# Expert stages of a two-layer diffusion backbone: TensorE's work written out in a fixed order, with the sums and picks of the second layer split and placed between the products

## The chip, the cores and the metric

One core of one Trainium2 chip. The metric is the device time of one execution in microseconds, as the median of three runs. All data are float32.

## The reference

Two layers work on 512 latent tokens (`x`) and 256 context tokens (`ctx`) of width 1024. Each layer is a mixer (mLSTM in layer 0, retention in layer 1) and then an expert-choice mixture of experts, cut here to what the change touches:

```python
def expert_choice_ffn(h, router, w_gate, w_up, w_down):
    cap = CAPACITY_FACTOR * t // N_EXPERTS              # 64 latent, 32 context tokens
    aff = softmax(h @ router)
    gate, idx = lax.top_k(swapaxes(aff, 1, 2), cap)     # each expert takes its best tokens
    xs = h[bidx, idx]
    hid = silu(xs @ w_gate) * (xs @ w_up)
    y = (hid @ w_down) * gate[..., None]
    return zeros_like(h).at[bidx, idx].add(y)
...
x = x + mod_l[5] * expert_choice_ffn(h_lat, ...)        # both layers
ctx = ctx + mod_c[5] * expert_choice_ffn(h_ctx, ...)    # layer 0 only
```

There are 16 experts a layer, each with three 1024 x 1024 matrices (12 MB). The second layer's result goes through a last RMSNorm.

## The kernel before, in words

`moe(l, ...)` (L1199) is the expert stage of layer `l`; its loop over the experts begins at L1488. The program is written in some order, and a scheduler puts each engine's instructions in its own order, from modelled times and from what each instruction needs. Where a block is under `tc.manual_schedule(engines={PE})`, TensorE keeps the written order; the other engines are still scheduled. Before the change only the first expert's opening (L1466) and the last expert (L1496) of layer 1 are under it.

**Weights.** `load` (L1165) fetches a 1 MB piece (256 rows of a matrix) on SP's queue. Gate, up and down of an expert are four pieces each. The pieces go round 19 slots in layer 0 and 14 in layer 1, and a load waits until the product that read its slot's last piece is done.

**Products.** `prod` (L1276) streams the weights past the chosen tokens: 32 matmuls of 512 columns for the 64 latent tokens, 64 of 256 columns for the 32 context tokens. `gate_up` (L1408) makes `gl` or `ul` (latent), or one half of `cg` (context: gate and up share one PSUM tile); after gate ScalarE takes Silu into `hid` (L1425), after up VectorE multiplies it (L1427). `turn` (L1429) transposes `hid` on TensorE (`hp`) and copies it on ScalarE into `hT`; `down` (L1437) makes `y`.

**Layer 0.** Tokens come by indirect DMA on POOL (`gather`, two experts ahead, three buffers `xg`) and the results are added in DRAM by indirect DMA, also on POOL. `prep` (L1225) transposes the next expert's tokens (`xp`) and modulates them on VectorE (`xs`, L1253 and L1255). In program order an expert is: `gl`, `cg` gate, `ul`, `cg` up, gathers, `prep` of the next, `turn` latent and context, `down` latent and context.

**Layer 1** (latent alone) keeps the tokens in SBUF. `select` (L1209) makes a 0/1 matrix `pick` for two experts at a time (`chosen` on TensorE, `own` and `pick` on VectorE); `prep`, called in odd experts for the next two, multiplies it with the tokens' high and low parts (`xr`, L1235, eight matmuls for each half of the width), copies to `rows` on ScalarE, transposes (`xp`, L1247) and modulates. `rows` and `hT` share one buffer (tag `hT0`). `put_back` (L1289) collects two experts' results (`o`), splits them into `bh` and `bl` after each odd expert, makes `put` matrices on VectorE and then, in one loop over four token tiles and two halves, adds them to the tokens: 16 matmuls `back` (L1313) into two PSUM buffers, eight adds on VectorE (L1316).

`xr`, `xp`, `hp` and `chosen` share three PSUM buffers (tag `tp`).

Of the kernel before, what the change touches and what calls it, by code (L numbers as in the profile page):

```python
# [9 lines left out]
F32 = mybir.dt.float32  # L10
# [3 lines left out]
AF = mybir.ActivationFunctionType  # L14
OP = mybir.AluOpType
# [8 lines left out]
NE = 16  # L24
# [3 lines left out]
LAT, CTX = 0, 1  # L28
# [16 lines left out]
def backbone(ctx, tc, x, c, ctx_in, c_ctx, ada_w, ada_b, norm_mix_g, norm_ffn_g, final_norm_g,  # L45
# [3 lines left out]
    nc = tc.nc  # L49
# [12 lines left out]
    ident = consts.tile([128, 128], F32, name="ident")  # L62
# [138 lines left out]
    def behind(late, early):  # L201

        for a in late:
            tc.add_manual_dep(a.ins, early.ins.name, mybir.DependencyInfo(mybir.DependencyClass.NoSync,
                                                                  mybir.DependencyReason.DATA), reason="order")
# [991 lines left out]
            return [lambda k, m=m: ws[m, k // 2][:, k % 2] for m in range(3)]  # L1197

    def moe(l, R, sb, sbx, late, mp, ml):  # L1199
        two = l == 0  # L1200
        NT = 96 if two else 128
        SPAN = ((0, 64), (64, 96)) if two else ((0, 128),)
# [22 lines left out]
        def prep(e, xs, parts):  # L1225

            a, b = SPAN[parts[0]][0], SPAN[parts[-1]][1]
            if l:
                pick = select(e)
            for hh in range(2):  # L1230
                if l:
                    p = mp.tile([128, 512], F32, name="xr", tag="tp", bufs=3)
                    for t in range(4):
                        for part in (R.XH, R.XL):
                            nc.tensor.matmul(p, pick[:, t, :], part[t][:, hh * 512:hh * 512 + 512],  # L1235
                                             start=(t == 0 and part is R.XH), stop=(t == 3 and part is R.XL))
                    rows_ = sb.tile([128, 512], F32, name="rows", tag="hT0", bufs=1)
                    nc.scalar.activation(rows_, p, AF.Copy)
                p = mp.tile([128, 4, NT], F32, name="xp", tag="tp", bufs=3)
                for kk in range(4):  # L1240
                    ks = slice((hh * 4 + kk) * 128, (hh * 4 + kk + 1) * 128)
                    if l == 0:
                        LATE["xp"] = nc.tensor.transpose(p[:, kk, a:b], R.XG[e][a:b, ks], ident[a:b, a:b])
                        if LATE.get("hold"):
                            behind([LATE["xp"]], LATE["hold"])
                    else:
                        nc.tensor.transpose(p[:, kk, :], rows_[:, kk * 128:(kk + 1) * 128], ident)  # L1247
                s = slice(hh * 4, hh * 4 + 4)
                for v in parts:
                    c0, c1 = SPAN[v]  # L1250
                    n = c1 - c0
                    o = xs[:, s, c0:c1] if xs.shape[2] == NT else xs[:, s, :]
                    nc.vector.tensor_tensor(o, p[:, :, c0:c1],  # L1253
                                            gsc[l][1][:, s, v:v + 1].to_broadcast([128, 4, n]), op=OP.mult)
                    LATE["xs"] = nc.vector.tensor_tensor(o, o,  # L1255
                                            modcol[l][:, 24 + hh * 4:28 + hh * 4, v:v + 1].to_broadcast([128, 4, n]),
                                            op=OP.add)

        def prep_first(xs, *groups):

# [28 lines left out]
        def put_back(e, o):  # L1289


            odd = e % 2
            if not odd:
                for q in range(2):
                    BACK[q] = sbx.tile([128, 512], F32, name=f"o{q}", bufs=1)
            for h in range(2):
                hs = slice(64 * h, 64 * h + 64)
                nc.vector.scalar_tensor_tensor(BACK[h ^ odd][hs, :], o[hs, :], R.gcol[hs, e:e + 1], M5[odd][hs, :],
                                               op0=OP.mult, op1=OP.mult)
            if not odd:  # L1300
                return
            put, hi, lo = [], [], []
            for q in range(2):
                hi.append(sbx.tile([128, 512], F32R, name=f"bh{q}", bufs=1))
                lo.append(sbx.tile([128, 512], F32R, name=f"bl{q}", bufs=1))
                split_piece(hi[q], lo[q], BACK[q])
                put.append(sb.tile([128, T_LAT], F32R, name=f"put{q}", bufs=1))
                nc.vector.tensor_scalar(put[q], R.tok, R.pair[:, q, e // 2:e // 2 + 1], None, op0=OP.is_equal)
            for t in range(4):
                for q in range(2):  # L1310
                    p = mp.tile([128, 512], F32, name="back", bufs=2)
                    for part in (hi, lo):
                        nc.tensor.matmul(p, put[q][:, t * 128:(t + 1) * 128], part[q],  # L1313
                                         start=part is hi, stop=part is lo)
                    xq = R.X[t][:, q * 512:(q + 1) * 512]
                    nc.vector.tensor_tensor(xq, xq, p, op=OP.add)  # L1316

# [25 lines left out]
        def final_gain():  # L1343

            fg = R.slot()[:, 0, :]
            for h in range(2):
                p = mp.tile([128, 4, 128], F32, name="rbp", tag="tp", bufs=3)
                for cc in range(4):
                    nc.tensor.transpose(p[:, cc, :], vc1[:, 80 + h * 4 + cc:81 + h * 4 + cc].to_broadcast([128, 128]),
                                        ident)  # L1350
                nc.scalar.activation(fg[:, h * 512:(h + 1) * 512], p.rearrange("p a b -> p (a b)"), AF.Copy)
            return fg
# [55 lines left out]
        def gate_up(v, xs, what, w, steps=range(8)):  # L1408
# [17 lines left out]
            else:  # L1426
                nc.vector.tensor_tensor(HID[v], HID[v], o, op=OP.mult)  # L1427

        def turn(v):  # L1429
            nb = 4 >> v  # L1430
            p = mp.tile([128, nb, 128], F32, name="hp", tag="tp", bufs=3)
            for cc in range(nb):
                nc.tensor.transpose(p[:, cc, :], HID[v][:, cc * 128:(cc + 1) * 128], ident)  # L1433
            HT[v] = (late if v else sb).tile([128, nb, 128], F32, name=f"hT{v}", bufs=1)
            LATE["act"] = nc.scalar.activation(HT[v], p, AF.Copy)  # L1435

        def down(v, e, w):  # L1437
            cw, nb = 64 >> v, 4 >> v
# [46 lines left out]
                R.ctx(mp)  # L1485
        M5 = gate_rows(l, late, mb0, mp) if two else R.M5

        for e in range(NE):  # L1488
            wg, wu, wd = W
            if two and e not in (0, NE - 1):  # L1490
                gate_up(LAT, xs, 0, wg)
                gate_up(CTX, xs, 0, wg)
                gate_up(LAT, xs, 1, wu)
                gate_up(CTX, xs, 1, wu)
            elif l and e == NE - 1:
                with tc.manual_schedule(engines={mybir.EngineType.PE}):  # L1496
                    fg = final_gain()
                    for what, w in enumerate((wg, wu)):
                        for b in range(4):
                            gate_up(LAT, xs, what, w, range(2 * b, 2 * b + 2))  # L1500
                            next(BACK["steps"], None)
                    turn(LAT)
                    finish(fg)
            elif not l or e:
                gate_up(LAT, xs, 0, wg)
                gate_up(LAT, xs, 1, wu)
            if e + 1 < NE:
                W = weights(e + 1)
                if two or e % 2:
                    xn = sbx.tile([128, 8, NT], F32, name="xs", bufs=2 - l)  # L1510
            if two and e == 0:
                turn(LAT)
                down(LAT, e, wd)
                LATE["hold"] = LATE["pe"]
                prep(0, xs, (CTX,))
                del LATE["hold"]
            if two and e in (0, NE - 1):
                if e:
                    turn(LAT)
                    down(LAT, e, wd)  # L1520
                    xc = sb.tile([128, 8, 32], F32, name="xc", tag="hT0", bufs=1)
                    prep(e, xc, (CTX,))
                    xs = xc
                gate_up(CTX, xs, 0, wg)
                gate_up(CTX, xs, 1, wu)
            if l == 0 and e + 2 < NE:
                for v in streams:
                    R.gather(e + 2, v)
            if e + 1 < NE and (two or e % 2):
                prep(e + 1, xn, streams if e + 2 < NE else (LAT,))  # L1530
            if e not in (0, NE - 1) or l and e == 0:
                turn(LAT)
            if two:
                turn(CTX)
            if e not in (0, NE - 1) or l and e == 0:
                down(LAT, e, wd)
            if two:
                down(CTX, e, wd)
            if two or e % 2:
                xs = xn  # L1540


    kn_scale = float(np.float32(128 ** -0.5))
# [328 lines left out]
```

## Time and profile before

| | us |
|---|---|
| median of 3 runs (lowest, highest) | 1977.88 (1977.67, 1979.93) |
| the profiled execution's own time | 1974.15 |
| its span, first to last instruction | 1972.4 |
| TensorE busy, share of the span | 1850.9, 94% |
| VectorE, ScalarE, GpSimd busy | 730.2, 426.8, 279.8 |
| moved by DMA | 585.42 MB, mean 297 GB/s |

Matmuls overlap in the array and their ends are modelled, so a busy TensorE need not be one at its peak. "Idle before" names what ended the idle time. In the rows, PE is TensorE, PEld its weight load, DVE VectorE, ACT ScalarE, POOL GpSimd and SP the engine that issues most transfers; SPq is its queue's own wait. DMA share is the busy share of 16 DMA engines from the time that packets took, so it can pass 1.

### The profile page before, as it was taken

The page shows a single profiled execution, that of the slowest core. Times are in us where ns is not written, and L with a number is a line of the kernel's source. Part 1 is how long each engine was busy: PE and PEld are TensorE (multiplying, and loading weights), DVE is VectorE, ACT ScalarE, POOL GpSimd, SP SyncE. Part 2 cuts the span into 40 slices and gives each one's busy share as a digit, 9 for nine tenths or more (in the row PEclk, how much of TensorE's full clock was granted, in tenths as well). Part 3 has the DMA queues.
Part 4 walks back from the last instruction along what each step waited for, and adds up shares of the span by engine and source line. Part 5 has one row for each costly group of instructions (what it writes and reads, how often), then busy time and mean ns, then how long its engine had stood idle before and what let it go on. Part 6 is the DMA issues. An engine that isn't in the chain of part 4 may idle for free. (4 is left out here: it accounts for less than half of the span.)

```text
span 1972.4 us, 27775 instructions
## 1 busy us (share of the span) xinstructions
PE 1850.9 (94%) x11091; PEld 1012.6 (51%) x11091; DVE 730.2 (37%) x1739; ACT 426.8 (22%) x839; POOL 279.8 (14%) x340
## 2 busy tenths in 40 slices
PE   7999988999999999999998999999979999989997
PEld 2765766787344443333334777788754333333332
DVE  3544567546111110110104677355551322222223
ACT  3532355432000000000004522322411000000001
POOL 1111133301211121120011124144000000000001
PEclk9999999999999999999999999999979999999999
DMA  8567776764999999999984588354559999999992
GB/s 285 205 209 268 253 207 196 230 228 144 333 393 375 391 383 384 383 382 393 401 319 126 182 279 276 112 173 150 208 208 395 415 416 414 415 414 414 416 413 86
DMA packets 218258, 585.42 MB, mean 297 GB/s; under 512 B 17674, under 2 KB 69618, under 8 KB 213010
## 3 DMA queue, kind: packets, MB, share of 16 engines
q1 hardware_dynamic: 209840, 570.72, 77.6%
q0 software_dynamic: 6912, 12.71, 3.2%
q8 instruction: 88, 1.44, 0.3%
q10 hardware_dynamic: 1378, 0.23, 0.1%
q14 instruction: 40, 0.33, 0.0%
HBM read 544.13 MB, written 39.47 MB: 296 GB/s over the span
## 5 line engine op out<-in xcount | busy, mean ns | idle before, releaser
L1282 PE MATMUL y<-wslot,hT 128*32 128x256 f32 (+1 forms) x2016 | 291.1, 488 | 9.8 <-ACT hT L1435 9.6
L1282 PE MATMUL gl<-wslot,xs 128*64 128x512 f32 x1024 | 260.3, 610 | 0.8 <-DVE xs L1255 0.8
L1282 PE MATMUL ul<-wslot,xs 128*64 128x512 f32 x1024 | 239.3, 596 | 0.0
L290 PE MATMUL acc<-whi,hT_hi 128*128 128x512 f32 x544 | 223.2, 411 | 4.8 <-ACT hT_hi L360 3.1
L291 PE MATMUL acc<-wlo,hT_hi 128*128 128x512 f32 x544 | 217.6, 400 | 0.3 <-POOL wlo L297 0.3
L292 PE MATMUL acc<-whi,hT_lo 128*128 128x512 f32 x544 | 217.3, 399 | 0.2 <-DVE hT_lo L361 0.2
L1427 DVE TENSOR_TENSOR hid<-hid,ul 128x512 f32<-128x512 f32 x32 | 22.0, 688 | 463.5 <-PE ul L1282 463.5
L1282 PEld LDWEIGHTS y<-wslot,hT 128*32 128x32 f32 (+1 forms) x2016 | 100.2, 123 | 178.1 <-issue 137.3
L1282 PEld LDWEIGHTS ul<-wslot,xs 128*64 128x64 f32 x1024 | 72.2, 137 | 140.8 <-issue 136.2
L1282 PEld LDWEIGHTS gl<-wslot,xs 128*64 128x64 f32 x1024 | 69.4, 138 | 135.5 <-issue 131.1
L290 PEld LDWEIGHTS acc<-whi,hT_hi 128*128 128x128 f32 x544 | 102.8, 189 | 39.4 <-issue 9.8
L1282 PE MATMUL cg<-wslot,xs 128*32 128x256 f32 x1920 | 118.9, 382 | 0.5 <-ACT hid L1425 0.5
L292 PEld LDWEIGHTS acc<-whi,hT_lo 128*128 128x128 f32 x544 | 102.8, 189 | 28.5 <-issue 4.9
L291 PEld LDWEIGHTS acc<-wlo,hT_hi 128*128 128x128 f32 x544 | 103.2, 190 | 23.7 <-issue 2.4
L1425 ACT ACTIVATE hid<-gl 128x512 f32<-128x512 f32 x32 | 19.1, 597 | 439.6 <-PE gl L1282 439.6
L297 DVE TENSOR_TENSOR wlo<-wslot,whi 128x512 fp32r<-128x512 f32 x108 | 80.6, 762 | 56.1 <-ACT whi L296 55.8
L1282 PEld LDWEIGHTS cg<-wslot,xs 128*32 128x32 f32 x1920 | 56.5, 109 | 84.1 <-issue 51.1
L296 ACT ACTIVATE whi<-wslot 128x512 fp32r<-128x512 f32 x112 | 69.4, 630 | 99.2 <-PE acc L292 98.2
L1435 ACT ACTIVATE hT<-hp 128x512 f32<-128x512 f32 (+1 forms) x48 | 23.7, 524 | 297.4 <-PE hp L1433 297.4
L1387 POOL TENSOR_TENSOR wslot<-x,wslot 128x512 f32<-128x512 f32 x4 | 5.0, 1271 | 493.2 <-DVE x L1330 491.6
L290 PE MATMUL po<-woh,yh 128*128 128x512 f32 x160 | 64.5, 403 | 3.2 <-ACT yh L923 3.2
L1449 DVE SCALAR_TENSOR_TENSOR o<-y,gcol,M 128x512 f32<-128x512 f32 (+1 forms) x32 | 19.8, 617 | 125.8 <-PE y L1282 125.8
(440 smaller groups left out, 2449.9 us busy)
## 6 DMA issues: line engine op xcount, KB each, us to landing
wslot<-in_moe_w_up_dram SPq DMA_DIRECT2D x128, 1024.0 KB
wslot<-in_moe_w_gate_dram SPq DMA_DIRECT2D x128, 1024.0 KB
wslot<-in_moe_w_down_dram SPq DMA_DIRECT2D x124, 1024.0 KB
wslot<-in_ada_w_dram SPq DMA_DIRECT2D x40, 1024.0 KB
wslot<-in_ret_w_in_dram SPq DMA_DIRECT2D x16, 1024.0 KB
wslot<-in_mlstm_w_in_dram SPq DMA_DIRECT2D x12, 1024.0 KB
wslot<-in_ada_w_dram SPq DMA_DIRECT2D x16, 512.0 KB
E<-rows_d SPq DMA_DIRECT2D x24, 256.0 KB
```

The source lines that it names most:

```text
L290: nc.tensor.matmul(o, lh, rh, start=first, stop=False)
L291: nc.tensor.matmul(o, lh, rl, start=False, stop=False)
L292: nc.tensor.matmul(o, ll, rh, start=False, stop=last)
L296: nc.scalar.activation(wh, w, AF.Copy)
L297: eng.tensor_tensor(wl, w, wh.bitcast(F32), op=OP.subtract)
L1282: mm = nc.tensor.matmul(o[cw * q:cw * q + cw, :], stat(k), w(k)[:, qn * n:(qn + 1) * n], start=(k == 0), stop=(k == 7), tile_position=(0, ...
L1387: nc.gpsimd.tensor_tensor(O[:, lo], R.X[t][:, lo], fg[:, lo], op=OP.mult)
L1425: nc.scalar.activation(HID[v], o, AF.Silu)
L1427: nc.vector.tensor_tensor(HID[v], HID[v], o, op=OP.mult)
L1435: LATE["act"] = nc.scalar.activation(HT[v], p, AF.Copy)
L1449: LATE["dve"] = nc.vector.scalar_tensor_tensor(r, o, TOP[v][2][:, e:e + 1], M5[v], op0=OP.mult, op1=OP.mult)
```

## The change

TensorE keeps the written order in experts 1 to 14 of layer 0 and in all of layer 1. The order itself is rewritten. In layer 0 the context's up product comes before the latent one, and `turn` and `down` take the context first. In layer 1 `prep` is cut into `pick_rows` (one half's `xr` and `rows`) and `row_columns` (that half's `xp` and `xs`), the sums of `put_back` into `add_back(tiles)`, and `turn` into its transposes and its copy; odd experts have the picks between their products, even ones the sums. What is computed stays the same.

```diff
 def moe(l, R, sb, sbx, late, mp, ml):
+    ordered = tc.manual_schedule
+    PE_ONLY = {mybir.EngineType.PE}
...
+    def pick_rows(e, hh):
+        pick = select(e)
+        p = mp.tile([128, 512], F32, name="xr", tag="tp", bufs=3)
+        for t in range(4):
+            for part in (R.XH, R.XL):
+                nc.tensor.matmul(p, pick[:, t, :], part[t][:, hh * 512:hh * 512 + 512], ...)
+        ROWS[hh] = sb.tile([128, 512], F32, name="rows", tag="hT0", bufs=1)
+        nc.scalar.activation(ROWS[hh], p, AF.Copy)
+
+    def row_columns(hh, xs):
+        p = mp.tile([128, 4, NT], F32, name="xp", tag="tp", bufs=3)
+        for kk in range(4):
+            nc.tensor.transpose(p[:, kk, :], ROWS[hh][:, kk * 128:(kk + 1) * 128], ident)
+        modulated(p, hh, xs, streams)
...
-        for t in range(4):
+    def add_back(*ts):
+        for t in ts if "put" in BACK else ():
             for q in range(2):
                 p = mp.tile([128, 512], F32, name="back", bufs=2)
...
     def turn(v):
+        turn_first(v)
+        turn_last(v)
...
+    region = ExitStack()
     for e in range(NE):
         wg, wu, wd = W
+        if e == 1 - l:
+            region.enter_context(ordered(engines=PE_ONLY))
+        if two and e == NE - 1:
+            region.close()
+        if l and e < NE - 1:
+            if e:
+                gate_up(LAT, xs, 0, wg)
+                if e % 2:
+                    pick_rows(e + 1, 0)
+                else:
+                    add_back(0, 1)
+                gate_up(LAT, xs, 1, wu)
+            W = weights(e + 1)
+            if e % 2:
+                xs = sbx.tile([128, 8, NT], F32, name="xs", bufs=1)
+                row_columns(0, xs)
+                pick_rows(e + 1, 1)
+                turn_first(LAT)
+                row_columns(1, xs)
+                turn_last(LAT)
+            else:
+                add_back(2)
+                if e + 2 < NE:
+                    select(e + 2)
+                turn_first(LAT)
+                add_back(3)
+                turn_last(LAT)
+            down(LAT, e, wd)
+            continue
         if two and e not in (0, NE - 1):
             gate_up(LAT, xs, 0, wg)
             gate_up(CTX, xs, 0, wg)
+            gate_up(CTX, xs, 1, wu)
             gate_up(LAT, xs, 1, wu)
-            gate_up(CTX, xs, 1, wu)
+            W = weights(e + 1)
+            xn = sbx.tile([128, 8, NT], F32, name="xs", bufs=2)
+            if e + 2 < NE:
+                for v in streams:
+                    R.gather(e + 2, v)
+            prep(e + 1, xn, streams if e + 2 < NE else (LAT,))
+            turn(CTX)
+            turn(LAT)
+            down(CTX, e, wd)
+            down(LAT, e, wd)
+            xs = xn
+            continue
...
+    region.close()
```

The last expert of layer 1 and the first and last of layer 0 are written as before, with the branches taken apart.

## Rows read from the trace of the kernel before

**Rows 1.** The page, slices of 49.3 us: GB/s that the DMA engines moved.

```profile
GB/s 285 205 209 268 253 207 196 230 228 144 333 393 375 391 383 384 383 382 393 401 319 126 182 279 276 112 173 150 208 208 395 415 416 414 415 414 414 416 413 86
```

**Rows 2.** Windows: us, busy (and count) of each engine, granted clock, DMA share, GB/s.

```profile
525.00:1000.00 475.00, 473.36 (x4098) 183.91 (x4090) 62.51 (x162) 24.45 (x53) 64.02 (x49) 1.00 1.03 386
1450.00:1475.00 25.00, 19.23 (x67) 12.08 (x69) 13.01 (x62) 2.11 (x4) 0.64 (x2) 0.67 0.47 184
1500.00:1925.00 425.00, 393.21 (x1708) 143.52 (x1706) 106.28 (x171) 34.98 (x58) 0.00 (x0) 1.00 1.03 414
1900.00:1925.00 25.00, 24.06 (x110) 8.13 (x108) 4.18 (x10) 2.28 (x4) 0.00 (x0) 1.00 1.03 410
1925.00:1950.00 25.00, 24.25 (x92) 6.99 (x90) 6.80 (x13) 1.19 (x2) 0.00 (x0) 1.00 0.15 55
```

**Rows 3.** Waits in layer 1, 1600:1905: who for whom, us in all, times, longest.

```profile
PE hp L1433 <- DVE hid L1427: 8.6, 10, 0.9
...
PE back L1313 <- ACT bh L296: 7.2, 5, 1.4
...
PE y L1282 <- ACT hT L1435: 5.4, 10, 0.7
...
PE xp L1247 <- ACT rows L1238: 3.8, 5, 0.8
...
SPq L1177 <- PE gl L1282: 112.4, 40, 5.7
```

**Rows 4.** The chain of waits in layer 1: start, us, what.

```profile
1660.86 6.88 PE ul L1282 x31
...
1671.91 1.13 PE xr L1235 x4
1673.04 1.87 PE y L1282 x8
...
1683.37 1.59 PE xr L1235 x6
...
1721.91 6.88 PE ul L1282 x31
...
1921.78 1.72 PE gl L1282 x8
```

**Rows 5.** TensorE's timeline in layer 0: start, us, what, count, [idle before].

```profile
565.88 7.08 PE L1282 MATMUL gl<-wslot,xs 128*64 128x512 f32 x30
...
737.23 7.09 PE L1282 MATMUL gl<-wslot,xs 128*64 128x512 f32 x32
...
758.45 0.88 PE L1243 MATMUL xp<-ident,xg 96*128 96x96 f32 x8
...
760.51 10.68 PE L1282 MATMUL y<-wslot,hT 128*64 128x512 f32 x96 [0.30 <-ACT hT L1435]
771.12 7.09 PE L1282 MATMUL gl<-wslot,xs 128*64 128x512 f32 x32
...
1028.85 7.09 PE L1282 MATMUL gl<-wslot,xs 128*64 128x512 f32 x32
```

**Rows 6.** TensorE's timeline in layer 0, a later expert.

```profile
881.60 1.94 PE L1282 MATMUL gl<-wslot,xs 128*64 128x512 f32 x8
883.47 1.07 PE L1282 MATMUL cg<-wslot,xs 128*32 128x256 f32 x16
...
918.71 1.94 PE L1282 MATMUL gl<-wslot,xs 128*64 128x512 f32 x8
```

**Rows 7.** TensorE's timeline, last expert of layer 0, and ahead of layer 1's experts.

```profile
1053.61 3.66 PE L1282 MATMUL cg<-wslot,xc 128*32 128x256 f32 x64 [1.46 <-DVE xc L1255]
1057.77 2.58 PE L1282 MATMUL cg<-wslot,xc 128*32 128x256 f32 x44 [0.51 <-ACT hid L1425]
...
1451.71 0.38 PE L993 MATMUL pl<-ident,af 128*16 128x128 f32 x1 [3.37 <-DVE af L992]
```

**Rows 8.** Groups by line on VectorE, 1660.8:1721.85: busy us, mean ns, idle before.

```profile
L1316 DVE TENSOR_TENSOR x<-x,back 128x512 f32<-128x512 f32 x8 | 5.2, 685 | 3.2 <-PE back L1313 3.2
```

More of the change, by code (lines that the diff above doesn't have):

```diff
@@ L1227, in prep @@
             a, b = SPAN[parts[0]][0], SPAN[parts[-1]][1]
-            if l:
-                pick = select(e)
             for hh in range(2):
-                if l:
-                    p = mp.tile([128, 512], F32, name="xr", tag="tp", bufs=3)
-                    for t in range(4):
[L1234 to L1238, printed above, removed]
                 p = mp.tile([128, 4, NT], F32, name="xp", tag="tp", bufs=3)
@@ L1241, in prep @@
                     ks = slice((hh * 4 + kk) * 128, (hh * 4 + kk + 1) * 128)
[L1242 to L1257, printed above, removed]
+                    LATE["xp"] = nc.tensor.transpose(p[:, kk, a:b], R.XG[e][a:b, ks], ident[a:b, a:b])
@@ new lines, in prep, with modulated @@
+                    if LATE.get("hold"):
+                        behind([LATE["xp"]], LATE["hold"])
+                modulated(p, hh, xs, parts)
+        def modulated(p, hh, xs, parts):
+            s = slice(hh * 4, hh * 4 + 4)
+            for v in parts:
+                c0, c1 = SPAN[v]
+                n = c1 - c0
+                o = xs[:, s, c0:c1] if xs.shape[2] == NT else xs[:, s, :]
+                nc.vector.tensor_tensor(o, p[:, :, c0:c1], gsc[l][1][:, s, v:v + 1].to_broadcast([128, 4, n]),
+                                        op=OP.mult)
+                LATE["xs"] = nc.vector.tensor_tensor(o, o, modcol[l][:, 24 + hh * 4:28 + hh * 4, v:v + 1]
+                                                     .to_broadcast([128, 4, n]), op=OP.add)
@@ new lines, in moe @@
+        ROWS = {}
+        def pick_rows(e, hh):
[3 more added lines that the diff above has]
+                for part in (R.XH, R.XL):
+                    nc.tensor.matmul(p, pick[:, t, :], part[t][:, hh * 512:hh * 512 + 512],
+                                     start=(t == 0 and part is R.XH), stop=(t == 3 and part is R.XL))
+            ROWS[hh] = sb.tile([128, 512], F32, name="rows", tag="hT0", bufs=1)
+            nc.scalar.activation(ROWS[hh], p, AF.Copy)
@@ L1301, in put_back @@
                 return
-            put, hi, lo = [], [], []
+            put, hi, lo = BACK["put"], BACK["hi"], BACK["lo"] = [], [], []
             for q in range(2):
@@ L1308, in put_back @@
                 nc.vector.tensor_scalar(put[q], R.tok, R.pair[:, q, e // 2:e // 2 + 1], None, op0=OP.is_equal)
-            for t in range(4):
+        def add_back(*ts):
+            for t in ts if "put" in BACK else ():
                 for q in range(2):
                     p = mp.tile([128, 512], F32, name="back", bufs=2)
-                    for part in (hi, lo):
-                        nc.tensor.matmul(p, put[q][:, t * 128:(t + 1) * 128], part[q],
-                                         start=part is hi, stop=part is lo)
+                    for part in ("hi", "lo"):
+                        nc.tensor.matmul(p, BACK["put"][q][:, t * 128:(t + 1) * 128], BACK[part][q],
+                                         start=part == "hi", stop=part == "lo")
                     xq = R.X[t][:, q * 512:(q + 1) * 512]
@@ L1427, in gate_up, with turn_first @@
                 nc.vector.tensor_tensor(HID[v], HID[v], o, op=OP.mult)
+        HP = {}
         def turn(v):
+            turn_first(v)
+            turn_last(v)
+        def turn_first(v):
             nb = 4 >> v
@@ L1433, in turn, with turn_last @@
                 nc.tensor.transpose(p[:, cc, :], HID[v][:, cc * 128:(cc + 1) * 128], ident)
-            HT[v] = (late if v else sb).tile([128, nb, 128], F32, name=f"hT{v}", bufs=1)
-            LATE["act"] = nc.scalar.activation(HT[v], p, AF.Copy)
+            HP[v] = p
+        def turn_last(v):
+            HT[v] = (late if v else sb).tile([128, 4 >> v, 128], F32, name=f"hT{v}", bufs=1)
+            LATE["act"] = nc.scalar.activation(HT[v], HP[v], AF.Copy)
         def down(v, e, w):
@@ L1492, in moe @@
                 gate_up(CTX, xs, 0, wg)
+                gate_up(CTX, xs, 1, wu)
                 gate_up(LAT, xs, 1, wu)
-                gate_up(CTX, xs, 1, wu)
[L1495 to L1507, printed above, removed]
-                W = weights(e + 1)
-                if two or e % 2:
-                    xn = sbx.tile([128, 8, NT], F32, name="xs", bufs=2 - l)
-            if two and e == 0:
+                W = weights(e + 1)
+                xn = sbx.tile([128, 8, NT], F32, name="xs", bufs=2)
[9 more added lines that the diff above has]
+                continue
+            if l:
+                fg = final_gain()
+                for what, w in enumerate((wg, wu)):
+                    for b in range(4):
+                        gate_up(LAT, xs, what, w, range(2 * b, 2 * b + 2))
+                        next(BACK["steps"], None)
+                turn(LAT)
+                finish(fg)
+                continue
+            gate_up(LAT, xs, 0, wg)
+            gate_up(LAT, xs, 1, wu)
+            if e == 0:
+                W = weights(e + 1)
+                xn = sbx.tile([128, 8, NT], F32, name="xs", bufs=2)
                 turn(LAT)
@@ L1516, in moe @@
                 del LATE["hold"]
[L1517 to L1526, printed above, removed]
+            else:
+                turn(LAT)
+                down(LAT, e, wd)
+                xs = sb.tile([128, 8, 32], F32, name="xc", tag="hT0", bufs=1)
+                prep(e, xs, (CTX,))
+            gate_up(CTX, xs, 0, wg)
+            gate_up(CTX, xs, 1, wu)
+            if e == 0:
                 for v in streams:
                     R.gather(e + 2, v)
[L1529 to L1539, printed above, removed]
+                prep(e + 1, xn, streams)
+            turn(CTX)
+            down(CTX, e, wd)
+            if e == 0:
                 xs = xn
+        region.close()
     kn_scale = float(np.float32(128 ** -0.5))
```

## The prediction

> **What bounds the kernel now.** I read the page's slices first. In the row of GB/s [rows 1] two stretches stand out, slices 11 to 20 and 31 to 39: the expert stages of layer 0 (about 380 to 400 GB/s) and of layer 1 (about 415). Nothing else in the kernel moves so much. Each streams 192 weight loads of 1 MB, so the first question is whether transfers or TensorE set the pace.
>
> The windows [rows 2] show both near their limit: TensorE is busy 473.4 of 475 us in layer 0 and 393 of 425 in layer 1, while the DMA share is 1.03 in both, at 386 and 414 GB/s. The waits decide it. In layer 1 TensorE never waits for a weight: its waits [rows 3] are for VectorE and ScalarE, in ten experts 8.6 us for `hid`, 7.2 for `bh`, 5.4 for `hT`, 3.8 for `rows`. The DMA queue waits instead, for TensorE to free a slot (112.4 us behind `gl` alone, more behind `y` and `ul`). So TensorE is the bound now, with transfers ahead of it.
>
> How far ahead matters, since that is all that a faster TensorE can use. In layer 1 the loads run at 414 GB/s to 1925 us; the 55 GB/s after that are 1.4 MB, so the last load lands at about 1928.4. Counting back eleven loads of 1.049 MB at 414 GB/s (2.53 us each), the first load of the last expert has landed at 1900.5. Its gate product starts at 1921.78 [rows 4]: a lead of 21.3 us. Two experts' weights need 25.17 MB / 414 GB/s = 60.8 us; two experts now take 1721.91 - 1660.86 = 61.05 us [rows 4]. The lead has therefore been nearly the same all along, and transfers are close behind as the next bound.
>
> **Layer 0, part by part.** The timeline of TensorE [rows 5] shows one expert with whole products, from `gl` at 737.23 to the next at 771.12: 33.89 us. The later experts are cut up: 8 `gl`, 16 `cg`, 8 `gl` and so on, 37.1 us from 881.60 to 918.71 [rows 6]. The work is the same; the difference is paid at the changes of shape. From the second expert's `gl` (565.9, less 0.4 for two matmuls done earlier) to the last one's (1028.85) are 463.4 us for 13 experts, 35.65 each.
>
> The fixed order makes all 13 whole. It also puts the context's up product right behind its gate product, in one PSUM tile, with nothing between. The last expert has them so now and shows the cost: up starts after a wait of 0.51 us for ScalarE's `hid` [rows 7]. So an expert costs 33.89 + 0.51 = 34.40 us. The tail from the first `xp` to the first `y`, 760.51 - 758.45 = 2.06 us [rows 5], I leave as it is. The latent up product comes last now, so its `hid` (0.69 us on VectorE, as for an add of that size [rows 8]) is done just as the transposes `xp` and the context's `hp` are, but VectorE then reaches `xs` later and gives back a `tp` buffer (three) later. Bounds: 0.3 us saved (the wait before `y`) to 0.7 lost per expert (one more VectorE operation in the way); I take nothing, as the nearest row has the same transposes and buffers. The gain is 13 x (35.65 - 34.40) = 16.3 us, between 7 and 20 by those bounds.
>
> Moved past the queues: gathers on POOL stay ahead of `prep`; the context's scatter now precedes the latent one, and nobody waits for either within the stage. Gate and up slots are given back later within an expert, which the lead covers. The transfers' pace in layer 0 (386 GB/s for 12.6 MB of weights plus the rows gathered and added, some 34 us an expert) is about that of the new order, so the lead holds.
>
> **Layer 1.** Per pair of experts:
> - Waits removed: 25.0 us in five pairs [rows 3], 5.0 a pair. Picks (`xr`) move between gate and up of the odd expert, sums (`back`) between gate and up of the even one and around its transposes, so that `hid`, `bh` and `hT` are made while TensorE has something to do.
> - Changes of shape removed: four `xr` take 1.13 us and six 1.59, so 0.23 each and 0.21 for getting in; the eight `y` after them take 1.87 instead of 8 x 6.88 / 32 = 1.72, so 0.15 for getting out [rows 4]. Of some eleven such insertions that the chain shows in a pair about five are left: 6 x 0.36 = 2.2 us.
> - Waits added: in the odd expert `hT` shares its buffer with `rows`, so its copy waits for the last `xp` and `y` for the copy: 0.7 us (the longest now [rows 3]). The second `rows` copy has only `hp` as cover: 0.2. Four `back` groups in a row have two PSUM buffers, and each is freed by an add of 0.69 us [rows 8]: between 0 and 1.4 us; I take 0.6, as the add of a group is only a little longer than the group. Together 1.5. The selection's mask sits behind the adds on VectorE, and only the next expert's pick needs it.
>
> TensorE then needs 61.05 - 5.0 - 2.2 + 1.5 = 55.35 us a pair, 5.7 less. Over seven pairs that is 40 us, but the lead is 21.3. Near the tenth expert it is used up, and from there TensorE waits for weights at 60.8 us a pair. The last expert's gate product can start at 1900.5 and everything after it follows as before. I take 20 us of the 21.3, as a load used when it lands costs a little at each product.
>
> Here a rule is weighed. The row says 414 GB/s, held over 425 us. The Trainium skill (DMA: Bandwidth & Descriptors, Where 436 GB/s comes from) says that transfers from HBM are bound by about 358 GB/s a core, with a fabric ceiling of 435. By 358 a pair would need 70.3 us (an estimate from that page): transfers would be the bound already and layer 1 would gain nothing; the trace refutes it. By 435 the floor would be 57.9 us, an estimate too, and layer 1 could gain about 39 us instead of 20.
>
> **Sum.** 16.3 + 20 = 36.3 us. The profiled execution took 1974.15 us (span 1972.4), so it would take 1937.9; the median of the runs shown is 3.7 us higher, and from it the forecast is 1977.9 - 36.3 = **1941.6 us**. Its own bounds: 7 to 20 in layer 0, 14 to 23 in layer 1, so 1935 to 1957.
>
> **Rivals.**
> - *The waits come back.* A fixed order can't fill a wait with other products. If VectorE's own order puts `xs` or the adds ahead of `hid`, layer 0 costs 34.9 us an expert (gain 13 x 0.75 = 9.7) and a pair in layer 1 59.5 (gain 10.5): 1958 us. For it: every wait in [rows 3] is for VectorE or ScalarE, whose order isn't fixed. Against it: both are mostly idle there.
> - *Transfers give more.* If loads that are freed earlier run faster, the cap moves and TensorE's own 40 us count in layer 1: 1977.9 - 16.3 - 40 = 1922 us. That takes 18.7 us more lead over seven pairs, so 58.1 us a pair or 433 GB/s. Against it: no slice shows more than 416 [rows 1], and the rate stands at 414 GB/s whatever TensorE waits for. The fabric ceiling of the page named above, 435 GB/s, would allow it.
> - *Slower: TensorE stands still for over 3 us in one piece in each expert of layer 1*, for example at a block of sums whose `bh` and `bl` aren't made yet. In the stretch from 1450 to 1475 us two such waits (the first is 3.37 us [rows 7]) go with a granted clock of 0.67 [rows 2]: one third of the stretch lost, 8.2 us, so 4.1 for each wait beside its own 3.2. At 7.3 us for each of 14 experts layer 1 loses 102 - 40 = 62 us, and with layer 0 the kernel takes 2024. It turns from gain to loss at about 8 of the 14 experts. Against it: the longest waits now are 0.7 to 1.4 us [rows 3] and the clock stays at 1.00 [rows 2]. The Trainium skill (TensorE: Matmul & The Clock Gate, Part 1) says that an idle TensorE falls to 1.2 GHz and recovers only with sustained work, which speaks against any order that waits; the two levels agree with the row.
> - *No change.* The scheduler keeps about this order, or the waits traded are equal: 1978 us.
>
> **Numbers.** Forecast 0.58, waits come back 0.22, transfers give more 0.05, slower by long waits 0.08, no change 0.07 (of that 0.02 slower by more than the bound). Faster by over 0.2% (4 us, about what can be told from no change): 0.58 + 0.22 + 0.05 = 0.85; same 0.05; slower 0.10. The range 1926 to 1964 takes in the forecast with its bounds and the first rival; the other three, 0.2 in all, lie outside.
>
> **What would show it.** Layer 0: `gl` to `gl` of 34.4 us in every expert from 2 to 14, a wait of about 0.5 us before the second `cg`, none above 0.4 before `y`. Layer 1: pairs of about 55 us up to the tenth expert, then about 60.8 with waits for weights at `gl`, `ul` and `y`; the DMA queue no longer waiting for slots there, still at 414 GB/s, and the last weights landing almost as long after the stage's start as now. The forecast is wrong if pairs stay above 59 us from the start, if weights come faster than 414 GB/s, or if the clock row leaves 1.00 in slices 11 to 20 or 31 to 39.

## The result, and the profile after

The kernel after takes 1943.59 us, the median of four runs (1941.18 to 1945.09). The kernel before, run beside it, takes 1977.78 (four runs, 1972.76 to 1979.93). The ratio is 0.983, with a 95% interval from 0.9808 to 0.9851: faster by 34.2 us, or 1.7%. The forecast was 1941.6, in a range from 1926 to 1964.

The profiled execution took 1944.39 us. Three lines of its page: the span, then, in 40 slices, the granted clock (in tenths of full speed, 9 being 90% or more) and the GB/s (those of before are [rows 1]):

```profile
span 1942.6 us, 27775 instructions
...
PEclk9999999999899999999999999999989999999999
...
GB/s 281 204 221 271 255 194 190 226 239 114 307 384 393 383 389 382 389 390 377 401 398 157 201 294 267 107 167 183 223 173 339 413 415 415 414 415 415 414 416 237
```

The two stretches at some 390 and 415 GB/s are the expert stages, as before. Neither runs faster; each is shorter.

To see where the time went, I cut both executions at three marks of TensorE's timeline: the first `gl` matmul of the first and of the last expert of layer 0, and the first of layer 1 (us):

| | up to the first expert | layer 0, first `gl` to the last expert's | to layer 1's first `gl` | from there to the end |
|---|---|---|---|---|
| before | 489.1 | 539.7 | 439.5 | 504.0 |
| after | 493.4 | 525.0 | 439.4 | 484.8 |

Layer 0 gave 14.7 us and layer 1 gave 19.2, together 33.9. The code ahead of the first expert is the same in both, but its time goes from 489 to 495 us over all the profiled executions below. So the two profiled executions differ by less (1974.15 - 1944.39 = 29.8 us) than the medians do.

**Layer 0.** One expert in TensorE's timeline (start, us, what, count, [idle before]); before, an expert looked like [rows 5] or, cut up, like [rows 6]:

```profile
880.57 7.04 PE L1292 MATMUL gl<-wslot,xs 128*64 128x512 f32 x32
887.54 3.66 PE L1292 MATMUL cg<-wslot,xs 128*32 128x256 f32 x64
891.70 3.66 PE L1292 MATMUL cg<-wslot,xs 128*32 128x256 f32 x64 [0.50 <-ACT hid L1438]
895.29 7.09 PE L1292 MATMUL ul<-wslot,xs 128*64 128x512 f32 x32
902.31 0.88 PE L1234 MATMUL xp<-ident,xg 96*128 96x96 f32 x8
903.03 0.38 PE L1452 MATMUL hp<-ident,hid 128*128 128x128 f32 x2
903.94 0.66 PE L1452 MATMUL hp<-ident,hid 128*128 128x128 f32 x4 [0.53 <-ACT hT L1457]
904.53 10.68 PE L1292 MATMUL y<-wslot,hT 128*32 128x256 f32 x96
915.04 5.32 PE L1292 MATMUL gl<-wslot,xs 128*64 128x512 f32 x24
```

All products are whole, and `gl` to `gl` takes 915.04 - 880.57 = 34.47 us. There are two waits, and the waits of the stretch from 525 to 1000 us (us in all, times, longest) show them in every expert:

```profile
PE cg L1292 <- ACT hid L1438: 7.0, 14, 0.5
PE hp L1452 <- ACT hT L1457: 6.9, 13, 0.5
```

The first was forecast. The second was not: the latent `hp` waits until ScalarE has copied the context's `hp` and so given back its `tp` buffer. In exchange the 0.30 us before `y` [rows 5] is gone.

**Layer 1.** The chain of waits (start, us, what). Before, no transfer was in it: it ran through TensorE and, in short steps, through the work of VectorE and ScalarE that TensorE waited for, 61.05 us a pair [rows 4]. After:

```profile
1515.39 6.87 PE gl L1292 x32
...
1569.78 6.87 PE gl L1292 x32
...
1624.17 6.87 PE gl L1292 x32
...
1647.31 17.97 DMA wslot<-in_moe_w_up_dram
1665.33 1.90 PE ul L1292 x7
1667.23 18.15 DMA wslot<-in_moe_w_gate_dram
...
1891.87 1.87 PE gl L1292 x8
```

Pairs take 54.4 us until the eighth expert. There the chain turns from TensorE to the weight transfers, and they carry it to the fifteenth expert; the pairs in that part, from `ul` to `ul`, take 60.2 to 61.5 us. The waits tell the same. First those from 1570 to 1650 us, to be read against [rows 3]:

```profile
PE y L1292 <- ACT hT L1457: 0.7, 1, 0.7
PE back L1326 <- DVE x L1329: 0.6, 2, 0.3
...
PE xp L1266 <- ACT rows L1261: 0.3, 1, 0.3
```

Then, from 1700 to 1890, those of TensorE for weights, which before had none, and the largest entry of the DMA queue (SPq):

```profile
PE gl L1292 <- DMA wslot<-in_moe_w_gate_dram: 10.6, 19, 0.7
...
PE ul L1292 <- DMA wslot<-in_moe_w_up_dram: 1.8, 3, 0.6
...
PE y L1292 <- DMA wslot<-in_moe_w_down_dram: 0.5, 2, 0.3
```

```profile
SPq L1177 <- PE y L1292: 29.8, 21, 2.7
```

The windows of both stages, with the columns of [rows 2]:

```profile
525.00:1000.00 475.00, 460.47 (x4250) 192.93 (x4244) 59.57 (x160) 27.23 (x56) 67.92 (x53) 1.00 1.03 386
...
1570.00:1650.00 80.00, 78.32 (x358) 30.58 (x356) 25.05 (x41) 7.31 (x12) 0.00 (x0) 1.00 1.03 415
...
1700.00:1875.00 175.00, 157.72 (x691) 57.02 (x691) 42.65 (x68) 14.36 (x24) 0.00 (x0) 1.00 1.03 415
```

In layer 0 TensorE is *less* busy than before (460.5 of 475 us against 473.4) and yet gets more done (4250 matmuls against 4098): the 3.2 us that an expert in pieces takes longer than a whole one [rows 5, 6] were counted as busy. Experiments 3 and 4 show that the pieces cost this; that it is paid at the changes of shape is the prediction's reading, which no run isolates. In layer 1 it is 98% busy in the early stretch and 90% in the late one, at the same DMA share and rate: the bound has changed hands in between.

### The profile page after: what moved, and what is told of

Its sections match the earlier page's. It is cut to its first block, busy times and chain, and to the rows that moved or that the text cites. A ratio compares the mean times of both kernels' runs of the same rounds, so it can differ in the third digit from the quotient of the medians.

```text
span 1942.6 us, 27775 instructions
## 1 busy us (share of the span) xinstructions
PE 1815.9 (93%) x11091; PEld 1023.0 (53%) x11091; DVE 729.1 (38%) x1739; ACT 428.5 (22%) x839; POOL 281.4 (14%) x340
## 5 line engine op out<-in xcount | busy, mean ns | idle before, releaser
L1292 PE MATMUL y<-wslot,hT 128*32 128x256 f32 (+1 forms) x2016 | 278.4, 486 | 8.2 <-ACT hT L1457 7.4
L1292 PE MATMUL gl<-wslot,xs 128*64 128x512 f32 x1024 | 237.1, 603 | 12.5 <-DMA wslot<-in_moe_w_gate_dram 11.7
L1292 PE MATMUL ul<-wslot,xs 128*64 128x512 f32 x1024 | 230.6, 596 | 2.5 <-DMA wslot<-in_moe_w_up_dram 2.2
L1292 PE MATMUL cg<-wslot,xs 128*32 128x256 f32 x1920 | 109.8, 380 | 7.6 <-ACT hid L1438 7.0
L1292 PEld LDWEIGHTS cg<-wslot,xs 128*32 128x32 f32 x1920 | 59.7, 110 | 62.3 <-ACT hid L1438 14.2
L1440 DVE TENSOR_TENSOR hid<-hid,cg 128x256 f32<-128x256 f32 x16 | 6.7, 420 | 203.4 <-PE cg L1292 203.4
```

The costliest lines, as they stand in the source:

```text
L1292: mm = nc.tensor.matmul(o[cw * q:cw * q + cw, :], stat(k), w(k)[:, qn * n:(qn + 1) * n], start=(k == 0), stop=(k == 7), tile_position=(0, ...
```

## Experiments

The change has two parts that can be had one without the other: the fixing (TensorE keeps the written order) and the rewriting of that order. Each can be had in one layer alone. The first four experiments were timed on one chip beside the kernel before at 1978.71 us (14 runs), the last four on another beside it at 1977.83 (9 runs).

**1. Layer 0 alone.** Layer 1 has its old order and is scheduled.

```diff
-            if e == 1 - l:
+            if two and e == 1 or l and e == NE - 1:
...
-                    row_columns(0, xs)
-                    pick_rows(e + 1, 1)
-                    turn_first(LAT)
-                    row_columns(1, xs)
-                    turn_last(LAT)
...
+                    for hh in range(2):
+                        pick_rows(e + 1, hh)
+                        row_columns(hh, xs)
+                turn(LAT)
...
+                if e % 2:
+                    add_back(0, 1, 2, 3)
```

> Layer 0's experts as after the change, layer 1's as before. Theory (the two layers gain independently: 13 experts at 34.47 instead of 35.65 us, and none of it is given back in between): 15 us faster than before, about 1963 us, and the span from layer 1's first gate product to the end as before, 504 us. Rival (layer 0's gain is lost, because the second mixer waits for something that doesn't come earlier): 1978.

Measured: 1960.68 us, ratio 0.9904 (0.9888 to 0.9921). Layer 0 takes 525.5 us between the marks, layer 1 503.1, as before the change.

**2. Layer 1 alone.** Layer 0 has its old order and is scheduled.

```diff
-            if e == 1 - l:
+            if l and e == 0:
...
-                gate_up(CTX, xs, 1, wu)
                 gate_up(LAT, xs, 1, wu)
+                gate_up(CTX, xs, 1, wu)
...
-                turn(CTX)
                 turn(LAT)
-                down(CTX, e, wd)
+                turn(CTX)
                 down(LAT, e, wd)
+                down(CTX, e, wd)
```

> Layer 1's experts as after the change, layer 0's as before. Theory: 19 us faster than before, about 1959 us, with waits for weights from the eighth expert on. Rival (layer 1's gain needs layer 0's, because the earlier end of layer 0 lets its first loads come earlier): under 10 us faster.

Measured: 1958.71 us, ratio 0.9897 (0.9878 to 0.9916). Layer 0 takes 540.4 us, layer 1 485.0. So the layers add up: 14.2 and 19.0 us by the marks, where the change gave 14.7 and 19.2. By the medians it is 18.0 and 20.0, together 38.0 against 34.2, within what the intervals allow.

**3. The old order, fixed.** The kernel before, with nothing changed but that TensorE keeps its program order in the same experts.

```diff
+            if e == 1 - l:
+                region.enter_context(tc.manual_schedule(engines={mybir.EngineType.PE}))
+            if two and e == NE - 1:
+                region.close()
```

> The program order of before, unchanged, but TensorE kept to it in the same experts as after the change. Theory (the fixing helps layer 0, where the written order is whole products with nothing waiting: 34.2 us an expert, gain 19; it harms layer 1, where the written order puts picks, sums and transposes one behind the other: about 64 us a pair instead of 61, loss 24, less what the lead of the loads covers, which is nothing on a slower TensorE): about 1982 us. Rival (the fixing alone does it and the rewritten order adds nothing): below 1950.

Measured: 1977.32 us (10 runs), ratio 0.9988 (0.9977 to 0.9999): 1.4 us, hardly clear of the noise. The marks show two large effects that cancel. Layer 0 takes 516.8 us, 22.9 less than before and 8.2 less than with the change. Layer 1 takes 526.0, which is 22.0 more. An expert of layer 0 in TensorE's timeline:

```profile
806.93 7.09 PE L1282 MATMUL gl<-wslot,xs 128*64 128x512 f32 x32
...
830.21 10.68 PE L1282 MATMUL y<-wslot,hT 128*64 128x512 f32 x96 [0.30 <-ACT hT L1435]
840.82 4.51 PE L1282 MATMUL gl<-wslot,xs 128*64 128x512 f32 x20
```

That is 33.89 us, with one wait of 0.30. In layer 1 (waits from 1600 to 1905, as in [rows 3]) the fixed old order can no longer put other work into its waits:

```profile
PE back L1313 <- ACT bh L296: 11.5, 5, 2.3
PE xp L1247 <- ACT rows L1238: 7.8, 10, 1.0
PE y L1282 <- ACT hT L1435: 7.5, 10, 0.7
PE xr L1235 <- DVE pick L1221: 5.2, 5, 1.0
PE hp L1433 <- DVE hid L1427: 3.4, 4, 0.9
PE back L1313 <- DVE bl L297: 1.1, 5, 0.2
PE back L1313 <- DVE x L1316: 0.9, 3, 0.3
```

These come to 37.4 us in five pairs, 7.5 a pair against 5.0 before. From `gl` to `gl` the pairs take 63.1 to 63.9 us; the first takes 70.3, where it took 60.5 before. The longest wait, 2.30 us in front of each block of sums, costs more than itself. The windows of the wait before one block and of the block's start (columns of [rows 2]):

```profile
1699.90:1702.25 2.35, 0.06 (x2) 0.00 (x1) 2.18 (x4) 1.26 (x2) 0.00 (x0) 1.00 1.03 413
1702.25:1706.00 3.75, 3.52 (x8) 2.01 (x8) 2.24 (x5) 0.00 (x0) 0.00 (x0) 0.60 1.03 411
```

Behind the wait the granted clock is 0.60 for 3.75 us, most of it at the 1.2 GHz level, so by estimate some 40% of 3.75, or 1.5 us, are lost beside the wait. What follows: in layer 0 the fixing is the whole gain, and the rewriting takes some of it back; in layer 1 the fixing alone loses what the rewriting has to win first.

**4. The new order, scheduled.** The written order of the change, but TensorE is fixed only where it was before.

```diff
-            if e == 1 - l:
+            if l and e == NE - 1:
```

> The program order of after, but the scheduler is free to reorder TensorE's work as before (only the last expert of layer 1 and its opening fixed). Theory (both are needed; the scheduler cuts the later experts of layer 0 up again and spreads sums and picks): layer 0 gains about 5 us of 15, layer 1 between 5 and 15 of 19: 1958 to 1968 us. Rival (the written order alone does it): 1944.

Measured: 1986.19 us (5 runs), ratio 1.0037 (1.0022 to 1.0052): slower than before, and slower than expected. Layer 1 gains 7.5 us (496.5, pairs of 60.1), but layer 0 loses 16.3 (556.0). Its first experts take 34.9 us, the late ones 38 to 41. The timeline shows a late one in pieces, as in [rows 6], now with a wait in its last part as well:

```profile
893.55 1.94 PE L1292 MATMUL gl<-wslot,xs 128*64 128x512 f32 x8
895.42 1.07 PE L1292 MATMUL cg<-wslot,xs 128*32 128x256 f32 x16
...
918.46 0.62 PE L1292 MATMUL y<-wslot,hT 128*32 128x256 f32 x2 [0.53 <-ACT hT L1457]
```

So the written order by itself is worth less than nothing over the whole kernel: the scheduler departs from it, and in layer 0 at a higher price than from the old one.

**5. Less work for TensorE in layer 1.** If weights set the pace from the eighth expert on, it must not matter. The low parts (`xl`, `bl`) are left out of the picks and sums: 4 matmuls in place of 8 for each half of the picks, 8 in place of 16 for the sums.

```diff
-                for part in (R.XH, R.XL):
+                for part in (R.XH,):
...
-                    for part in ("hi", "lo"):
-                        nc.tensor.matmul(p, BACK["put"][q][:, t * 128:(t + 1) * 128], BACK[part][q],
-                                         start=part == "hi", stop=part == "lo")
+                    nc.tensor.matmul(p, BACK["put"][q][:, t * 128:(t + 1) * 128], BACK["hi"][q], start=True, stop=True)
```

> After, with the products with the low parts left out of layer 1's picks and sums (16 matmuls less in each pair of experts, 3.8 us of TensorE). Theory (from the eighth expert on weights set layer 1's pace): the first pairs take about 50.5 us instead of 54.4, the lead is used up two experts sooner, and the pairs behind it still take 61: the stage's span stays at 485 us within 2, the whole at 1943. Rival (TensorE's own work sets the end): 7 x 3.8 = 26 us less, about 1917.

Measured: 1947.01 us in one run, layer 1 484.7 us (with the change 484.8). The first pairs are shorter (51.5 us), the chain turns to the transfers two experts sooner, in the sixth, and the later pairs are as long as ever (59.2 to 62.2). The chain and the window:

```profile
1490.50 6.87 PE gl L1292 x32
...
1542.04 6.87 PE gl L1292 x32
...
1588.49 18.64 DMA wslot<-in_moe_w_up_dram
```

```profile
1700.00:1875.00 175.00, 150.40 (x647) 49.14 (x645) 43.37 (x70) 14.53 (x24) 0.00 (x0) 1.00 1.03 414
```

TensorE has 7.3 us less to do in this stretch than with the change and waits that much longer, at the same 414 GB/s.

**6. Fewer bytes in layer 1.** The counterpart: of each `down` piece of experts 2 to 13 half is left out, and the half that is loaded is used twice, so TensorE does as much work as before on fewer bytes.

```diff
+            elif self.l and 2 <= e <= 13 and m == 2:
+                nc.sync.dma_start(w[:, 0], dram_ap(w_down, off + b * 256 * D, [[D, 128], [1, D]]))
+                w = w[:, 0:1].to_broadcast([128, 2, D])
```

> After, with only half of each down piece loaded for experts 2 to 13 of layer 1 (its products read that half twice): 10 instead of 12 MB an expert, TensorE's work as it was. Theory (weights set the pace): all pairs take TensorE's own 54.4 us, and the last expert starts some 25 us earlier: about 1919 us, the stage's span 459. Rival (something else, such as waits that appear late in the stage, makes the later pairs 61 us): 1943.

Measured: 1918.86 us in one run. Layer 1 takes 462.7 us, 22.1 less than with the change, and six pairs in a row take 54.4, by the chain from 1512.51 to 1838.81. Its window shows TensorE as the bound again and the transfers below their rate:

```profile
1512.51 6.87 PE gl L1295 x32
...
1838.81 6.87 PE gl L1295 x32
```

```profile
1700.00:1875.00 175.00, 170.89 (x776) 66.14 (x772) 46.47 (x74) 15.62 (x26) 0.00 (x0) 1.00 1.00 391
```

Both are single runs, but chain, window and stage agree, and together they settle the cap: the new order is good for 54.4 us a pair through the whole stage, and the weights keep it from that.

**7. Layer 0 in its old order, fixed; layer 1 as changed.** Experiments 1 to 3 say that this should beat the change.

```diff
-                gate_up(CTX, xs, 1, wu)
                 gate_up(LAT, xs, 1, wu)
+                gate_up(CTX, xs, 1, wu)
...
-                turn(CTX)
                 turn(LAT)
-                down(CTX, e, wd)
+                turn(CTX)
                 down(LAT, e, wd)
+                down(CTX, e, wd)
```

> TensorE fixed in both layers, layer 1 in the order of after, layer 0 in the written order of before (context up last, latent turned first). Theory (from the run with the old order fixed: 33.9 us an expert instead of 34.5; the up product of the context right behind its gate product costs 0.5 us an expert, and turning the context first 0.5 more, of which it saves 0.3): 8 us faster than after, about 1935 us. Rival (with layer 1 faster too, transfers eat it): 1943.

Measured: 1936.81 us (5 runs, 1933.51 to 1941.66), ratio to before 0.9802 (0.9781 to 0.9823). Layer 0 takes 515.9 us, 9.1 less than with the change, and layer 1 484.2.

**8. The same, with the latent `turn` ahead of `prep`.** One wait of 0.30 us is left in an expert of layer 0: `y` for its `hT`. If `hid` is turned before the next expert's tokens, their transposes cover the copy.

```diff
+                turn(LAT)
                 prep(e + 1, xn, streams if e + 2 < NE else (LAT,))
                 turn(CTX)
-                turn(LAT)
-                down(CTX, e, wd)
                 down(LAT, e, wd)
+                down(CTX, e, wd)
```

> As the run with layer 0 in the order of before, but with the latent hidden tile turned ahead of the next expert's transposes, so that these cover the copy that the down product waits for. Theory: the wait of 0.3 us before y goes, 33.6 us an expert, 4 us faster than that run, about 1931 us. Rival (the third transpose buffer is taken, and the wait moves to the context's transposes): as that run, 1935.

Measured: 1935.43 us (5 runs, 1931.33 to 1939.51), ratio to before 0.9796 (0.9777 to 0.9815). Layer 0 takes 514.0 us. TensorE's timeline has no wait left in the expert, which takes 835.79 - 802.19 = 33.60 us:

```profile
802.19 7.09 PE L1292 MATMUL gl<-wslot,xs 128*64 128x512 f32 x32
...
823.41 0.66 PE L1452 MATMUL hp<-ident,hid 128*128 128x128 f32 x4
823.90 0.83 PE L1234 MATMUL xp<-ident,xg 96*128 96x96 f32 x8
824.81 0.44 PE L1452 MATMUL hp<-ident,hid 128*128 128x128 f32 x2
825.18 10.68 PE L1292 MATMUL y<-wslot,hT 128*64 128x512 f32 x96
835.79 7.09 PE L1292 MATMUL gl<-wslot,xs 128*64 128x512 f32 x32
```

By its median this is the best version, 8 us ahead of the change, but the two were timed apart and their intervals against the kernel before overlap; the marks give 525.0 - 514.0 = 11.0 us in layer 0. The 1.4 us between experiments 7 and 8 are less than their runs spread; only the timeline and the marks show that gain.

## Why the prediction was right

**Layer 0, 16.3 us forecast, 14.7 measured.** The step "33.89 + 0.51" holds for its parts: the products are whole, and the wait before the second `cg` is 0.50. The term that I left as it was, the tail from `xp` to `y`, was a little mis-sized: 904.53 - 902.31 = 2.22 us in place of 2.06. The wait before `y` went, as the better of its two bounds had it, but the latent `hp` came in with 0.53, behind ScalarE's copy; the text had looked for a late buffer at VectorE. An expert takes 34.47 us where 34.40 were forecast, which is 0.9 of the 1.6 us missing. The rest lies in the first expert, whose order was not fixed: up to the second expert's `gl` it takes 77.0 us, before 76.3.

What the prediction did not ask is which half of the edit brings this. Its own terms had the answer, 33.89 us for whole products and 0.51 on top for the rewriting, but it took the gain as one. Experiments 3 and 7 show that fixing brings 22.9 us and that rewriting costs 8 of them, (34.47 - 33.89) x 13 = 7.5 by the timeline. The number came out, but the design it was worked out for is not the better one.

**Layer 1, 20 us forecast, 19.2 measured.** The deciding step, that the lead of the loads (21.3 us) caps the gain, is shown by experiments 5 and 6. The pair was forecast at 55.35 and takes 54.4. The waits added were sized well: in a pair 0.7 for `hT`, 0.3 for `rows` and 0.3 for a `back` buffer, 1.3 in all against 1.5. The changes of shape were mis-sized: without its waits a pair took 61.05 - 5.0 = 56.05 us of TensorE before [rows 3, 4] and takes 54.4 - 1.3 = 53.1 now, so 3.0 us of them went and not 2.2. With the shorter pair the lead lasts 21.3 / (60.8 - 54.4) = 3.3 pairs and not 3.9, and it was used up at the eighth expert rather than "near the tenth"; the sum did not depend on it. The last weights land as late in the stage as forecast: this window after [rows 2] is the one in which they end,

```profile
1900.00:1925.00 25.00, 24.25 (x90) 7.11 (x90) 8.68 (x16) 2.32 (x5) 1.16 (x1) 1.00 0.72 278
```

and 25 x 278 / 415 = 16.7 us into it is 1916.7, or 458.9 us after the stage's first `gl` (1457.8). Before it was 1928.4 - 1468.3 = 460.1.

**Two signs did not hold.** The text expected "the DMA queue no longer waiting for slots there". It still waits, 29.8 us behind `y` alone, in waits of up to 2.7 us. With transfers as the bound the queue of issues still runs ahead of them (in the chain above a load takes some 18 us, while one lands every 2.53), so that a wait of the issuing queue alone does not say who is the bound; the rate and the waits of TensorE do. The text also named a clock below 1.00 in slices 11 to 20 as a sign of being wrong, and the clock row has an 8 in slice 11. That is the opening of the first expert, with four waits of 0.69 to 1.50 us ahead of its `gl`: the granted clock is 0.90 from 480 to 490 us and 0.59 from 490 to 500. Before, with the same four waits some 4 us earlier, it was 0.67 and 0.81 in these windows, so the change did not bring it; the sign was drawn too wide.

**Base.** Taking the sum from the median, and not from the profiled execution 3.7 us below it, was right: that execution was short in the stretch that nobody changed (489.1 us, against 490.4 to 495.0 in the other nine).

**The rivals.** *The waits come back*: not here; it asked for 34.9 us an expert and 59.5 a pair. A new wait of 0.53 did come in layer 0, but the old one of 0.30 left. Its mechanism is at work in experiment 3, where an order that was not made for fixing pays 63 us a pair. *Transfers give more*: refuted, 413 to 416 GB/s in each slice; the ceiling of 435 from the Trainium skill (DMA: Bandwidth & Descriptors, Where 436 GB/s comes from) is reached in no run here, and its bound of 358 is passed in all. *Slower by long waits*: not here, as no wait of TensorE in layer 1's pairs is over 0.75 us and the clock stays at 1.00. But the mechanism exists, at the very place that the rival named, the sums that wait for `bh`: experiment 3 has it, at 2.3 us of wait and some 1.5 of clock rather than the 3.2 and 4.1 taken from [rows 2, 7]. The rule cited there, that an idle TensorE falls to 1.2 GHz (the Trainium skill, TensorE: Matmul & The Clock Gate, Part 1), agrees with that window. *No change*: this is what experiment 3 gives.

## What to carry to other kernels

Where a scheduler cuts products into pieces, test the fixing of the order and the rewriting of it apart, stage by stage: here each alone is worth next to nothing or less over the whole kernel, in one stage the fixing is all of the gain, and in the other it harms until the order is made for it. Before counting a saved wait, work out the lead of the next resource in line; it caps the gain however well the waits are removed. And when two streams share a stage, look at what a new neighbour waits for: a second half of one PSUM tile, or the copy that gives back the last buffer of a pool.

## What the runs showed of the hardware

Between the products of layer 1 short waits did not lower TensorE's clock, however many there were, and single ones of 2.3 us did. In the late part of layer 1 TensorE was idle for 17.3 of 175 us in waits of at most 0.75 us, in experiment 5 for 24.6 us in waits of at most 0.8, and the granted clock was 1.00 in both. In experiment 3 one wait of 2.30 us, behind a stretch at 1.00, left it at 0.60 for the next 3.75 us; in that run's windows from 1560 to 1905 us the clock is 0.93 to 0.97 wherever a block of sums lies, and 1.00 from 1650 to 1700, where none does. Length alone does not decide it: at the opening of layer 0 four waits of at most 1.50 us within 8 us went with 0.59. I had looked only for waits of over 3 us.

The rate of the weight transfers did not move with what they fed. In layer 1 it was 413 to 416 GB/s whether TensorE or the weights were the bound, before, with the change and in experiment 5. It was lower where TensorE never waited for a weight and gave back slots more slowly than transfers fill them: 391 GB/s in experiment 6, at a DMA share of 1.00 in place of 1.03, and 389 to 398 in the windows of experiment 3 with a block of sums.
